# Sums of x's blocks pinned behind the steps for 1/rms, in a decoder step on one core

## The chip, the cores and the metric

The program runs on one core of one Trainium2 chip. The time is device microseconds of one execution, taken as the median of several runs. The engines are named as the profile names them: PE (TensorE) multiplies matrices, with PEld for the loading of its stationary operand; DVE (VectorE) and ACT (ScalarE) work on rows of 128 partitions; POOL (GpSimd) and SP (SyncE) here mostly issue DMAs. Matmul results arrive in PSUM and have to be read from there by DVE or ACT; everything else stands in SBUF.

## The reference

One inference step of a decoder with two layers, for 512 prompt tokens and 8 sample tokens at once, so 520 columns, model width 1024. Each layer is

```
x += 0.5 * swiglu(rms(x))
x += mixer(rms(x))          # pooling in layer 0, windowed attention in layer 1
x += 0.5 * swiglu(rms(x))

rms(x)    = x * rsqrt(mean(x*x) + 1e-5) * g
swiglu(h) = (silu(h @ w_gate) * (h @ w_up)) @ w_down        # 1024 -> 2816 -> 1024
```

So there are four feed-forward networks (FFN 0 to 3). Between FFN 1 and FFN 2 the keys and values are projected once from rms(x), with rotary positions on the keys. A final rms ends it. All numbers are float32.

## The kernel before

**Layout.** x is held transposed, as eight blocks of 128 channels by 520 tokens. Since 1/rms belongs to a token, and a token is a column, it can be multiplied in after a matrix product instead of before it: products are formed from x times g, and their result is multiplied by R, a tile that holds 1/rms of each token in all 128 partitions. So a product can start before R is known, but its result can't be used before.

**Matmuls.** Each float32 operand is split into a high and a low part (`split`, L238: ACT writes the high one at L242, DVE the low one at L243), and a product is made of three terms. Weights are split the same way (ACT L191, DVE L192) some pieces ahead of their use, and the columns go in two halves of 260. One matmul of the traces is 128 by 128 by 260.

**The two kinds of tile.** Each FFN makes 22 column tiles of the hidden width. A plain tile (`plain_tile`, 96 matmuls, L412) forms gate and up in two PSUM tiles, then DVE multiplies gate by R (L470), ACT takes silu, DVE multiplies by up (L472), and `hidden` splits the result for the down projection. A Strassen tile (`strassen_tile`, 84 matmuls, L437) needs seven products instead of eight. It needs sums and differences of x's blocks (`sums`, L515, in a dictionary `tt`, with parts th and tl), and sums of weights, for which a further piece S is loaded and added in by DMA and DVE (L155 to L165). The first `NPL[fi]` tiles of an FFN are plain, two in each; the sums of x's blocks are made meanwhile.

**1/rms.** The squares (ACT L363) are added up over x's eight blocks by DVE in `acc` (L367). `rstd_tok` multiplies acc by a column of ones on PE (L378), which gives the sum for each token, and then twelve DVE operations on 128 by 5 numbers (L382 to L389) make 1/rms from it by an initial guess and three Newton steps, as `r_tok`, one token to a partition. `rstd_all` spreads it over all partitions: DVE makes a diagonal matrix of r_tok's column (L397, L399), PE multiplies it by a matrix of ones (L398, L400), ACT copies the result to R (L401, L402).

**What sets the order.** Engines work off their queues in order, and run beside each other as semaphores let them. The order within a queue is made by a planner from a cost model when the program is built, except for instructions wrapped in `later`, which keep the place that the program gives them. In an FFN the steps above are called as hooks, one after each weight piece of the plain tiles (`start_hooks`, L592): a step of the sums, `rstd_tok`, `rstd_all`, then eight more steps of the sums.

**Elsewhere.** `kv_pass` runs the keys and then the values. During the keys it calls `rstd_tok` after block 1 and `rstd_all` after block 3, and the sums of FFN 2 are made during the values. `rope` (L821) turns the keys, in kv, and the queries, in attention: ACT copies the result out of PSUM (L825), DVE multiplies the PSUM result by cosines (L826), shuffles the copy, multiplies it by sines (L828) and adds. In attention `rstd_tok` and `rstd_all` stand between parts of the query projection. PSUM has four tiles of two banks each for all of this.

Of the kernel before, what the change touches and what calls it, by code (L numbers as in the profile page):

```python
# [28 lines left out]
LAG = 2  # L29
NPL = (2, 2, 2, 2)  # L30
HD = 64
# [178 lines left out]
def yoco_step(ctx, tc, ins, outs):  # L210
# [161 lines left out]
    def rstd_tok():  # L372
# [8 lines left out]
        t1 = cp.tile([P, 5], F32, tag="nt", name="nt")  # L381
        V.tensor_scalar(v, pss[:, :5], 1.0 / D, EPS, op0=ALU.mult, op1=ALU.add)  # L382
        V.tensor_scalar(y.bitcast(I32), v.bitcast(I32), 1, None, op0=ALU.arith_shift_right)
# [6 lines left out]

    def rstd_all(pool):

        dg2 = pool.tile([P, NS], F32, tag="dg2", name="dg2", bufs=1)
        pr, pr2 = pss_[0][:, 1, :], pss_[0][:, 0, 8 : 8 + NS]
        for t in range(4):
            dg = pool.tile([P, P], F32, tag="dg", name="dg", bufs=4)
            V.tensor_scalar(dg, ident, r_tok[:, t : t + 1], None, op0=ALU.mult)  # L397
            T.matmul(pr[:, t * P : (t + 1) * P], ones, dg, start=True, stop=True)  # L398
        V.tensor_scalar(dg2, ident[:, 112:120], r_tok[:, 4:5], None, op0=ALU.mult)  # L399
        T.matmul(pr2, ones, dg2, start=True, stop=True)  # L400
        S.copy(R[:, :SP], pr)  # L401
        S.copy(R[:, SP:], pr2)  # L402
# [48 lines left out]
    class Hidden(list):  # L451


        def __init__(self, tags):
            self.tags = tags

    def plain_tile(tmp, mov, hs, hooks):

        pg, pu = duo(), duo()
        for k0 in (0, 4):  # L460
            for banks in (pg, pu):
                w = W.get()
                W.prefetch()
                for k in range(k0, k0 + 4):
                    mm(w, k - k0, mov[k], banks, k == 0, k == KT - 1)
                if hooks:
                    hooks.pop(0)()
        g = tmp.tile([P, TOK], F32, tag="g", name="g")
        t = tmp.tile([P, TOK], F32, tag="t", name="t")
        V.tensor_tensor(halves(g), pg[:, :, :H], halves(R), op=ALU.mult)  # L470
        S.activation(t, g, AF.Silu)
        V.scalar_tensor_tensor(halves(g), pu[:, :, :H], -1.0, halves(t), op0=ALU.mult, op1=ALU.mult)  # L472
        hidden(g, hs)

# [40 lines left out]
    def sums(tmp, n, tt):  # L515


        for k in range(4):
# [7 lines left out]
            t1, t2, t3, t4 = hcols(t12, 0), hcols(t12, 1), hcols(t34, 0), hcols(t34, 1)  # L526
            V.tensor_tensor(t1, b11, b12, op=ALU.subtract)
            V.scalar_tensor_tensor(t2, t1, -1.0, b22, op0=ALU.mult, op1=ALU.subtract)
            tt[k] = pair(TT, [P, TOK])
            split(tt[k], t12)  # L530
            yield
            V.tensor_tensor(t3, b22, b12, op=ALU.subtract)
            V.scalar_tensor_tensor(t4, t2, -1.0, b21, op0=ALU.mult, op1=ALU.subtract)
# [57 lines left out]

    def start_hooks(tmp, n, tt):  # L592

        steps = sums(tmp, n, tt)
        step = lambda: next(steps, None)
        return [step, rstd_tok, lambda: rstd_all(tmp)] + [step] * 8


    mov1 = []
    with ff_pool() as tmp:  # L600
# [95 lines left out]

        ffn(0, tmp, mov0, start_hooks(tmp, 0, tt), tt, HH, deferred(1, tmp, "g", XX, mov1, TW), pool_prep())

# [97 lines left out]
    with ff_pool() as tmp:  # L796
# [11 lines left out]
        tt = {}  # L808
        ffn(1, tmp, mov2, start_hooks(tmp, 2, tt), tt, HH, deferred(N_KV, tmp, "g", XX, movk))

# [9 lines left out]
    def rope(out, banks, cosr, sinr, pool, tags):  # L820
# [4 lines left out]
        S.copy(halves(raw), banks[:, :, :H])  # L825
        V.tensor_tensor(halves(out), banks[:, :, :H], halves(cosr), op=ALU.mult)  # L826
        V.stream_shuffle(sw, raw, swap)
# [5 lines left out]
    with ff_pool() as tmp:  # L833
# [22 lines left out]
        def during_k(k):  # L856
            if k == 1:
                rstd_tok()
            if k == 3:
                rstd_all(tmp)  # L860

# [50 lines left out]
    with tc.tile_pool(name="at", bufs=2) as at:  # L912
# [158 lines left out]
        q_part(1, 0)  # L1071
        rstd_all(at)
        q_part(1, 1)
# [139 lines left out]
    with ff_pool() as tmp:  # L1213
# [29 lines left out]

        ffn(3, tmp, mov6, start_hooks(tmp, 5, tt), tt, HH, final_after)
        turn(*waiting.pop())
# [46 lines left out]
```

## Time and profile before

| | us |
|---|---|
| median of 3 runs | 1743.63 |
| lowest and highest run | 1741.86, 1750.61 |
| the profiled execution | 1745.72 |
| its span, first to last instruction | 1744.0 |
| mean granted TensorE clock in it | 0.973 |

The page of the profile gives the busy time of each engine and its share of the span, the span in 40 slices, and the chain of waits that ended last. The timeline lists single instructions or runs of the same one, with start, length and, in brackets, the idle time before it and what ended that. The windows view sums busy time by engine over a stretch. The granted clock is the share of full speed at which PE was let run; where it is 0.5, a matmul takes twice as long.

### The profile page before, as it was taken

To read this page: it belongs to the slowest core of one execution; us is meant where nothing else is said; L and a number is where in the kernel's file an instruction comes from. 1 tells how busy PE (TensorE), PEld (TensorE's weight loads), DVE (VectorE), ACT (ScalarE), POOL (GpSimd) and SP (SyncE) were. 2 spreads that over 40 slices of the span, in tenths; PEclk is the share of its full clock that TensorE was granted. 3 is DMA by queue.
4 is the path that set the end of the run, shared out by engine and by line. 5 is a ranking of instruction groups with operands and counts; after the bars stand their busy time and mean duration, and the time that the engine had idled before them with its cause. 6 is when DMAs were issued, how large, how long until landed. Compare 5 with 4: busy or idle time off the path is not lost.

```text
span 1744.0 us, 34399 instructions
## 1 busy us (share of the span) xinstructions
PE 1667.9 (96%) x13689; PEld 1655.0 (95%) x13689; DVE 1275.7 (73%) x2487; ACT 909.5 (52%) x1812; POOL 147.8 (8%) x180
## 2 busy tenths in 40 slices
PE   5999999999899999998999999998889899999996
PEld 5999999999899999998999999998879899999996
DVE  7775866878775875887775875888756785785775
ACT  6553643666552652654552643656766663463453
POOL 1001101001001101100101101100000110110100
PEclk8999999999899999998999999999979999999998
DMA  9445746653355755643645845642112465675621
GB/s 225 115 134 134 178 132 141 177 171 105 85 151 128 167 148 135 150 133 93 149 139 133 185 134 133 166 138 70 35 25 73 104 151 146 138 177 140 151 86 50
DMA packets 316687, 227.85 MB, mean 131 GB/s; under 512 B 9312, under 2 KB 291528, under 8 KB 316486
## 3 DMA queue, kind: packets, MB, share of 16 engines
q1 hardware_dynamic: 286400, 175.08, 35.2%
q0 software_dynamic: 23488, 42.34, 14.9%
q10 hardware_dynamic: 6638, 8.23, 1.5%
q8 instruction: 107, 1.75, 0.4%
q14 instruction: 54, 0.44, 0.1%
HBM read 181.16 MB, written 5.04 MB: 107 GB/s over the span
## 4 chain that ended last, share of the span: by engine, by line
PE 88%; DVE 6%; ACT 3%; DMA 2%; issue 1%; SPq 0%; ACTq 0%; DVEq 0%
PE ps L437 46%; PE ps L412 37%; DVE sm L990 1%; DVE wl L192 1%; PE ps L720 1%; PE ps L1046 1%; ACT sm L1005 1%; DMA pr<-in_bands_dram 1%; PE ps L745 1%; PE ps L378 0%; ACT wh L191 0%; PE ps L398 0%; DVE xl L243 0%; DMA S<-in_ffn_w_up_dram 0%; DVE tl L243 0%
## 5 line engine op out<-in xcount | busy, mean ns | idle before, releaser
L191 ACT ACTIVATE wh<-raw 128x512 fp32r<-128x512 f32 (+1 forms) x744 | 452.0, 623 | 566.7 <-PE ps L412 348.5
L192 DVE TENSOR_TENSOR wl<-raw,wh 128x512 fp32r<-128x512 f32 (+1 forms) x744 | 492.9, 678 | 219.5 <-ACT wh L191 209.7
L437 PE MATMUL ps<-tl,wh 128*128 128x260 f32 x1280 | 361.4, 282 | 0.0
L437 PE MATMUL ps<-th,wh 128*128 128x260 f32 x1280 | 360.9, 282 | 0.0
L437 PE MATMUL ps<-th,wl 128*128 128x260 f32 x1280 | 359.2, 282 | 0.0
L412 PE MATMUL ps<-hh,wh 128*128 128x260 f32 x1376 | 281.5, 285 | 3.6 <-DVE mx L990 2.2
L412 PE MATMUL ps<-hl,wh 128*128 128x260 f32 x1376 | 281.0, 283 | 0.0
L412 PE MATMUL ps<-hh,wl 128*128 128x260 f32 x1376 | 279.2, 283 | 0.0
L437 PEld LDWEIGHTS ps<-tl,wh 128*128 128x128 f32 x1280 | 241.0, 188 | 0.0
L437 PEld LDWEIGHTS ps<-th,wh 128*128 128x128 f32 x1280 | 240.8, 188 | 0.0
L437 PEld LDWEIGHTS ps<-th,wl 128*128 128x128 f32 x1280 | 240.1, 188 | 0.0
L412 PEld LDWEIGHTS ps<-hh,wh 128*128 128x128 f32 x1376 | 212.8, 189 | 5.0 <-DVE mx L990 2.9
L412 PEld LDWEIGHTS ps<-hl,wh 128*128 128x128 f32 x1376 | 214.8, 190 | 0.0
L412 PEld LDWEIGHTS ps<-hh,wl 128*128 128x128 f32 x1376 | 213.6, 189 | 0.0
L437 PE MATMUL ps<-xl,wh 128*128 128x260 f32 x720 | 201.6, 283 | 0.0
L437 PE MATMUL ps<-xh,wh 128*128 128x260 f32 x720 | 201.5, 282 | 0.0
L437 PE MATMUL ps<-xh,wl 128*128 128x260 f32 x720 | 197.5, 282 | 0.0
L156 POOL DMA_DIRECT2D raw<-raw x80 | 69.3, 866 | 1398.8 <-DVE wl L192 558.8
L571 DVE TENSOR_TENSOR u<-ps,R 128x520 f32<-128x520 f32 x96 | 67.1, 700 | 107.0 <-PE ps L412 107.0
L437 PEld LDWEIGHTS ps<-xl,wh 128*128 128x128 f32 x720 | 135.5, 188 | 0.0
L437 PEld LDWEIGHTS ps<-xh,wh 128*128 128x128 f32 x720 | 135.4, 188 | 0.0
L437 PEld LDWEIGHTS ps<-xh,wl 128*128 128x128 f32 x720 | 133.4, 188 | 0.0
(233 smaller groups left out, 2840.1 us busy)
## 6 DMA issues: line engine op xcount, KB each, us to landing
raw<-in_ffn_w_gate_dram SPq DMA_DIRECT2D x87, 512.0 KB, 4.0
raw<-in_ffn_w_up_dram SPq DMA_DIRECT2D x87, 512.0 KB, 5.8
raw<-in_ffn_w_down_dram SPq DMA_DIRECT2D x32, 1024.0 KB, 5.1
S<-in_ffn_w_up_dram SPq DMA_DIRECT2D x80, 256.0 KB, 5.5
raw<-raw POOLq DMA_DIRECT2D x80, 256.0 KB, 3.3
S<-raw POOLq DMA_DIRECT2D x80, 256.0 KB, 4.7
raw<-in_ffn_w_down_dram SPq DMA_DIRECT2D x16, 768.0 KB, 4.2
raw<-in_w_q_dram SPq DMA_DIRECT2D x8, 512.0 KB, 3.8
```

Source lines behind the costliest of these rows:

```text
L156: G.dma_start(blk(raw, 2, 1), blk(raw, 1, 1), accum_op=ALU.add)
L191: nc.scalar.activation(dh, src, AF.Copy)
L192: nc.vector.tensor_tensor(dl, src, dh.bitcast(F32), op=ALU.subtract)
L412: T.matmul(banks[:, hf, :H], a[:, kk, :], hcols(b, hf), start=(first and i == 0), stop=(last and i == 2),)
L437: T.matmul(bank[:, :H], a[:, kk, :], b, start=(not more and kk == 0 and i == 0), stop=(kk == 3 and i == 2), skip_group_check=more,)
L571: V.tensor_tensor(halves(u), banks[m][:, :, :H], halves(R), op=ALU.mult)
L720: T.matmul(o, a[:, s], b[:, kk, :], start=(n == 0), stop=(n == 5))
L745: T.matmul(po[:, half * 256 : half * 256 + 256], z[:, tau, c], b, start=(i == 0), stop=(i == len(lst) - 1),)
L990: V.tensor_tensor_reduce(out=sm[:, e * 256 : (e + 1) * 256], in0=self.pe[e][:, bi * 256 : (bi + 1) * 256], in1=cst[:, mk : mk + 256], op0= ...
L1005: S.activation(part(i), part(i), AF.Exp, bias=nm[:, i : i + 1], accum_out=den[:, i : i + 1])
L1046: T.matmul(po[:, bi * 256 : (bi + 1) * 256], a, p_[:, kc_], start=(n == 0), stop=(n == 3 * len(kts) - 1),)
```

## The change

1. FFN 0 has three plain tiles instead of two (so one Strassen tile less); the others keep two.
2. `later` pins the first of the twelve operations for r_tok, and the first subtract of each of the eight sums, in program order. In `start_hooks` the hook calls are rearranged: none for the first one or two weight pieces (`late`: 2 in FFN 0 and 1, 1 in FFN 3), then `rstd_tok` with a step of the sums behind it, none, `rstd_all`, and the other seven steps.
3. `rstd_all` makes no diagonal. r_tok's column, repeated 128 times along the free axis, is the stationary operand, and the identity the moving one. 25 DVE operations go.
4. A plain tile that ends before `rstd_all` was called is copied out of PSUM by ACT (two copies), and its remaining steps, as operations from SBUF, are put off until R is known. In the built program that holds for the first tile of FFN 0 and the first of FFN 1.
5. In `rope` the product with the cosines reads ACT's copy instead of PSUM.

```diff
-NPL = (2, 2, 2, 2)
+NPL = (3, 2, 2, 2)
...
-        V.tensor_scalar(v, pss[:, :5], 1.0 / D, EPS, op0=ALU.mult, op1=ALU.add)
+        later(V.tensor_scalar(v, pss[:, :5], 1.0 / D, EPS, op0=ALU.mult, op1=ALU.add))
...
-    def rstd_all(pool):
+    def rstd_all():
-        dg2 = pool.tile([P, NS], F32, tag="dg2", name="dg2", bufs=1)
         pr, pr2 = pss_[0][:, 1, :], pss_[0][:, 0, 8 : 8 + NS]
         for t in range(4):
-            dg = pool.tile([P, P], F32, tag="dg", name="dg", bufs=4)
-            V.tensor_scalar(dg, ident, r_tok[:, t : t + 1], None, op0=ALU.mult)
-            T.matmul(pr[:, t * P : (t + 1) * P], ones, dg, start=True, stop=True)
-        V.tensor_scalar(dg2, ident[:, 112:120], r_tok[:, 4:5], None, op0=ALU.mult)
-        T.matmul(pr2, ones, dg2, start=True, stop=True)
+            T.matmul(
+                pr[:, t * P : (t + 1) * P], r_tok[:, t : t + 1].broadcast_to([P, P]), ident, start=True, stop=True
+            )
+        T.matmul(pr2, r_tok[:, 4:5].broadcast_to([P, P]), ident[:, 112:120], start=True, stop=True)
         S.copy(R[:, :SP], pr)
         S.copy(R[:, SP:], pr2)
...
+    copied, there = [], [False]
+
+    def known():
+        there[0] = True
+        while copied:
+            copied.pop(0)()
...
         g = tmp.tile([P, TOK], F32, tag="g", name="g")
         t = tmp.tile([P, TOK], F32, tag="t", name="t")
-        V.tensor_tensor(halves(g), pg[:, :, :H], halves(R), op=ALU.mult)
-        S.activation(t, g, AF.Silu)
-        V.scalar_tensor_tensor(halves(g), pu[:, :, :H], -1.0, halves(t), op0=ALU.mult, op1=ALU.mult)
-        hidden(g, hs)
+        if not there[0]:
+            S.copy(halves(g), pg[:, :, :H])
+            S.copy(halves(t), pu[:, :, :H])
+
+            def rest():
+                V.tensor_tensor(g, g, R, op=ALU.mult)
+                S.activation(g, g, AF.Silu)
+                V.scalar_tensor_tensor(g, t, -1.0, g, op0=ALU.mult, op1=ALU.mult)
+                hidden(g, hs)
+
+            copied.append(rest)
+        else:
+            V.tensor_tensor(halves(g), pg[:, :, :H], halves(R), op=ALU.mult)
+            S.activation(t, g, AF.Silu)
+            V.scalar_tensor_tensor(halves(g), pu[:, :, :H], -1.0, halves(t), op0=ALU.mult, op1=ALU.mult)
+            hidden(g, hs)
...
-            V.tensor_tensor(t1, b11, b12, op=ALU.subtract)
+            later(V.tensor_tensor(t1, b11, b12, op=ALU.subtract))
...
-            V.tensor_tensor(t3, b22, b12, op=ALU.subtract)
+            later(V.tensor_tensor(t3, b22, b12, op=ALU.subtract))
...
-    def start_hooks(tmp, n, tt):
+    def start_hooks(tmp, n, tt, late):
         steps = sums(tmp, n, tt)
         step = lambda: next(steps, None)
-        return [step, rstd_tok, lambda: rstd_all(tmp)] + [step] * 8
+        there[0] = False
+        none = lambda: None
+
+        def norm():
+            rstd_tok()
+            step()
+
+        def norm_all():
+            rstd_all()
+            known()
+
+        return [none] * late + [norm, none, norm_all] + [step] * 7
...
-        ffn(0, tmp, mov0, start_hooks(tmp, 0, tt), tt, HH, deferred(1, tmp, "g", XX, mov1, TW), pool_prep())
+        ffn(0, tmp, mov0, start_hooks(tmp, 0, tt, 2), tt, HH, deferred(1, tmp, "g", XX, mov1, TW), pool_prep())
...
-        ffn(1, tmp, mov2, start_hooks(tmp, 2, tt), tt, HH, deferred(N_KV, tmp, "g", XX, movk))
+        ffn(1, tmp, mov2, start_hooks(tmp, 2, tt, 2), tt, HH, deferred(N_KV, tmp, "g", XX, movk))
...
         S.copy(halves(raw), banks[:, :, :H])
-        V.tensor_tensor(halves(out), banks[:, :, :H], halves(cosr), op=ALU.mult)
+        V.tensor_tensor(out, raw, cosr, op=ALU.mult)
...
-        ffn(3, tmp, mov6, start_hooks(tmp, 5, tt), tt, HH, final_after)
+        ffn(3, tmp, mov6, start_hooks(tmp, 5, tt, 1), tt, HH, final_after)
```

In kv and in attention only the calls of `rstd_all` lose their argument; the pin inside `rstd_tok` and the spread act there too.

More of the change, by code (lines that the diff above doesn't have):

```diff
@@ L859, in during_k @@
             if k == 3:
-                rstd_all(tmp)
+                rstd_all()
         mov3, tt = [], {}
@@ L1071, in yoco_step @@
         q_part(1, 0)
-        rstd_all(at)
+        rstd_all()
         q_part(1, 1)
```

## The prediction

> **What bounds the kernel now.** I read the page first, then the chain of waits, then the timeline and windows of the places where TensorE (PE) stands idle.
>
> ```profile
> PE 1667.9 (96%) x13689; PEld 1655.0 (95%) x13689; DVE 1275.7 (73%) x2487; ACT 909.5 (52%) x1812; POOL 147.8 (8%) x180
> PEclk8999999999899999998999999999979999999998
> PE 88%; DVE 6%; ACT 3%; DMA 2%; issue 1%; SPq 0%; ACTq 0%; DVEq 0%
> ```
>
> PE is busy 96% of the span and holds 88% of the chain that ended last. So there are two ways to gain: fewer matmuls, or fewer of the remaining idle stretches. One stretch of the chain gives the price of a matmul when nothing waits:
>
> ```profile
> 55.55 54.53 PE ps L437 x456
> ```
>
> 54.53/456 = 0.1196 us. A Strassen tile (84 matmuls) costs 10.05 us, a plain tile (96) 11.48.
>
> The idle lies at the starts: where 1/rms is formed and spread before the first plain tile's result may be scaled. Timeline of the first FFN (start, length, engine, operation; in brackets the idle before it and its releaser):
>
> ```profile
> 33.34 0.63 ACT L191 ACTIVATE wh<-S 128x512 fp32r<-128x512 f32 x1 [4.60 <-DMA S<-raw]
> 37.11 0.70 DVE L367 TENSOR_TENSOR acc<-acc,sq 128x520 f32<-128x520 f32 x1
> 37.95 2.26 PE L378 MATMUL ps<-ones,acc 128*128 128x1 f32 x10 [9.93 <-DVE acc L367]
> 55.39 0.28 PE L437 MATMUL ps<-xh,wh 128*128 128x260 f32 x1
> ```
>
> PE stands 9.93 us (from 28.02) for the sum of squares. That sum is late because ACT, with the last squares queued behind, waits 4.60 us for a weight sum S by DMA, which only a Strassen tile needs. The other starts:
>
> ```profile
> 430.68 1.17 PE L378 MATMUL ps<-ones,acc 128*128 128x1 f32 x10
> 444.49 2.04 PE L398 MATMUL ps<-dg,ones 128*128 128x128 f32 x8 [6.78 <-ACT th L242]
> 447.50 0.80 PE L412 MATMUL ps<-xh,wh 128*128 128x260 f32 x2 [0.74 <-ACT R L402]
> 455.98 0.28 PE L437 MATMUL ps<-xh,wh 128*128 128x260 f32 x1
> ...
> 807.76 2.05 PE L398 MATMUL ps<-dg,ones 128*128 128x128 f32 x8 [6.44 <-ACT th L242]
> ...
> 1382.09 2.05 PE L398 MATMUL ps<-dg,ones 128*128 128x128 f32 x8 [3.96 <-issue]
> 1392.56 0.28 PE L437 MATMUL ps<-xh,wh 128*128 128x260 f32 x1
> ```
>
> ACT's th is named as releaser, but PE really waits for the DVE chain that makes r_tok, since DVE mixes the twelve tiny steps with the sums of x's blocks:
>
> ```profile
> 431.89 0.17 DVE L382 TENSOR_SCALAR nv<-ps 128x5 f32<-128x5 f32 x1
> 437.48 0.70 DVE L243 TENSOR_TENSOR tl<-t,th 128x520 fp32r<-128x520 f32 x1
> 438.09 0.16 DVE L387 SCALAR_TENSOR_TENSOR nt<-nt,nv 128x5 f32<-128x5 f32 x1
> 438.16 0.43 DVE L528 SCALAR_TENSOR_TENSOR t<-t,xb 128x260 f32<-128x260 f32 x1
> 438.50 0.43 DVE L532 TENSOR_TENSOR t<-xb,xa 128x260 f32<-128x260 f32 x1
> 443.59 0.17 DVE L389 SCALAR_TENSOR_TENSOR r_tok<-nt,ny 128x5 f32<-128x5 f32 x1
> ...
> 1178.94 0.15 DVE L382 TENSOR_SCALAR nv<-ps 128x5 f32<-128x5 f32 x1
> 1181.15 0.17 DVE L389 SCALAR_TENSOR_TENSOR r_tok<-nt,ny 128x5 f32<-128x5 f32 x1
> ```
>
> The chain lasts 11.87 us in the second FFN, and 2.38 in attention where hardly anything stands between. The same rows give DVE's pace: 0.61 from a long operation to the next, 0.34 from a short one.
>
> How much of each start is waiting, by the windows view (length; busy time and count by engine; granted clock; DMA share; GB/s):
>
> ```profile
> core 0: us, PE busy (x) PEld busy (x) DVE busy (x) ACT busy (x) POOL busy (x), PEclk, DMA share, GB/s
> 28.00:56.00 28.00, 17.33 (x123) 17.24 (x123) 20.66 (x52) 14.57 (x25) 2.64 (x3) 0.76 0.45 97
> 419.00:456.00 37.00, 29.47 (x216) 29.20 (x216) 29.67 (x78) 21.58 (x37) 3.69 (x5) 0.82 0.30 67
> 794.00:843.00 49.00, 41.82 (x326) 41.47 (x325) 31.05 (x70) 21.67 (x39) 7.45 (x10) 0.90 0.51 119
> 1367.00:1393.00 26.00, 21.30 (x156) 21.02 (x155) 18.82 (x50) 14.97 (x25) 2.60 (x3) 0.87 0.41 93
> ```
>
> At 0.1196 each, 216, 326 and 156 matmuls are 25.8, 39.0 and 18.7 us; the windows last 11.2, 10.0 and 7.3 longer. That bounds what these three starts can give back, lost clock included.
>
> **A gap also costs clock.** The pooling step shows what follows a short one, and the change leaves short ones:
>
> ```profile
> 386.07 0.28 PE L720 MATMUL ps<-tl,xh 128*128 128x256 f32 x1
> 390.58 1.25 PE L378 MATMUL ps<-ones,acc 128*128 128x1 f32 x10 [2.70 <-DVE acc L367]
> 392.25 0.42 PE L720 MATMUL ps<-th,xh 128*128 128x256 f32 x1
> 390.00:395.00 5.00, 4.42 (x26) 4.45 (x27) 2.86 (x15) 3.00 (x10) 1.77 (x2) 0.70 0.78 257
> ```
>
> After 2.70 us of idle the same matmul takes 0.42 instead of 0.28 and the clock of the window is 0.70, so 0.30 x 5 = 1.5 us are lost there; with what spills into the next window I take 1.7 for each start that keeps a gap. [...]
>
> **The change, part by part.**
>
> First FFN. With a third plain tile the early weights need no S, so the 4.60 us wait of ACT goes from ahead of the squares. By the order in which the changed program was built, what stands before the last square is two weight splits and one copy of a finished tile; I put the last square at about 29.5, acc at 30.6 and L378 at 30.75, an idle of 2.7 instead of 9.93. Then L378 (1.17), 31 matmuls, the spread (1.03), 161 matmuls: 192 x 0.1196 = 23.0, and Strassen starts at 55.9, against 55.39. But one more of the 22 tiles is done by then: 10.05 - 0.5 = 9.6 gained, less the clock of 1.7: **7.9**. The 12 more matmuls are in it. The 31 matmuls (3.7 us) cover the r_tok chain (2.4). Sums follow the chain on DVE, by my count done at 57 to 59, about when product two asks for them; 3 us later would cost 3: ends 5 and 9.6.
>
> The copying: ACT takes both results of a tile out before R is known, four copies in two tiles, each about
>
> ```profile
> 794.30 0.57 ACT L825 COPY rp<-ps 128x520 f32<-128x520 f32 x1
> 1188.12 0.70 DVE L826 TENSOR_TENSOR qT<-ps,xh 128x520 f32<-128x520 f32 x1
> 1188.73 0.69 DVE L828 TENSOR_TENSOR rp<-rp,xl 128x520 f32<-128x520 f32 x1
> ```
>
> 0.57, one of them ahead of the last square (counted). It frees the PSUM banks early, so PE need not stop for R. The product that finishes the tile later, and rope's first product, read SBUF instead of PSUM: 0.69 against 0.70, nothing. In rope the keys' banks come free with the copy, without R.
>
> Spread without the diagonal: five times 5 DVE operations go, all off PE's path once DVE is not late, so nothing by themselves. The stationary operand is now one column repeated 128 times. No row shows such a load. Nearest:
>
> ```profile
> L398 PEld LDWEIGHTS ps<-dg,ones 128*128 128x128 f32 x40 | 7.3, 273 | 17.7 <-issue 10.8 <-ACT th L242 7.0
> ```
>
> 273 ns now. I take the same; if it were free the 40 would give 7.3 at most (all exposed), if twice as slow cost 10.9 more.
>
> Second FFN. The pin holds L382 and its eleven successors ahead of the sums: 431.9 + 2.4 + one long operation = r_tok at 434.9, instead of 443.59. PE has 49 matmuls (5.9 us) behind L378, to 437.7: no wait for R, and without waits it reaches Strassen at 444.2 instead of 455.98. Now the sums are late: behind r_tok DVE has 15 short and 21 long operations plus 1.0 of small copies of the sinks, 15 x 0.34 + 21 x 0.61 + 1.0 = 18.9, to 453.8, with the last ACT hop 455.4. PE gets 36 to 48 matmuls in meanwhile, waiting for one sum after the other. At 456.9 I count 60 Strassen matmuls where before had 8: 52 x 0.1196 = 6.2, less 1.7: **4.5**. Ends: 2 if the sums come 2.5 later, 11.2 if they never count.
>
> Keys and values. 103 matmuls (12.3 us) now lie between L378 and the spread, so the idle goes: up to 10.0. But the third weight piece's low part stands on DVE behind cs, kT and rp, two each at 0.61 and over, which wait for R (about 809.4): ready at 814.3, while PE asks at 811.1: 3.2 back, and 1.7 of clock: **5.1**. Ends 2 and 10. The chain itself isn't shortened here; 14 other operations still stand between its steps.
>
> Attention: the spread comes after 50 matmuls instead of 57; PE had no wait there, so R 0.9 earlier may shorten what waits for it: 0.5, ends -2 and 3.
>
> Fourth FFN. r_tok at 1368.1 + 3.0 = 1371.1 instead of 1381.5; 15 short and 22 long (18.5), 2.8 of waits for R and banks and one ACT hop put the last sum at about 1393.4. PE would be there at 1385.2. At 1394.4 I count 48 done against 15: 3.9 - 1.7 = **2.2**. Ends 0 and 7.3.
>
> What the pin adds as a wait: DVE stands at L382 for PE, with all sums and weight low parts behind it. Before, that wait was
>
> ```profile
> 795.49 0.17 DVE L382 TENSOR_SCALAR nv<-ps 128x5 f32<-128x5 f32 x1 [0.37 <-PE ps L378]
> ```
>
> 0.37, and L378 keeps its place in PE's order in every start (96 matmuls before it in both FFNs with 96 before), so I count the same. Queues: SP issues one DMA less and POOL two less, nothing else is moved past another there.
>
> Sum: 7.9 + 4.5 + 5.1 + 0.5 + 2.2 = 20.2. The profiled execution took 1745.72, so 1725.5; it lies 2.1 above the median of the runs (1743.63), so **1723** in terms of the median. Own range of this case 1717 to 1730.
>
> **Rivals.** (1) The short gaps leave the clock alone, or are shorter than I think. Four times 1.7 comes back: gain 27.0, 1716.6. For it: no row shows where below 2.70 us the loss begins, and my gaps may come out shorter; against: the row of 390.58. [...] (2) DVE becomes the bound in the starts: every sum also needs an ACT pass between its DVE steps (th, about 0.6) which DVE exposes when it has nothing else. Four sums by 0.87 make 3.5 more in each of three starts, 10.4: gain 9.8, 1734. For it: DVE is busy 29.67 of 37 us in 419 to 456; against: weight work lies between to fill the hops. (3) The planner's order makes nothing of it: what is gained in a start is taken back by the next weight's wait (DMA share 0.45 in 28 to 56, so no bound is near): 1743. (4) Slower: DVE stands at L382 while PE is late at L378, with the sums and the low parts of the weights that PE needs next behind it. Each start then ends d later, where d is that wait. It turns the sign at d = 20.2/4 = 5.1 us and shows as slower from (20.2 + 8.7)/4 = 7.2; at the 9.93 of today's first gap, 4 x 9.93 = 39.7, less 20.2: 1763. Against: the 0.37 above, and no row of the other starts with an idle before L378.
>
> **How the numbers follow.** The forecast gets 0.58, rival 1 0.15, 2 0.15, 3 0.05, 4 0.07. Half a per cent, about what a measurement can tell, is 8.7 us: faster is below 1734.9. That takes nearly all of the forecast (0.57) and of rival 1 (0.15), and over half of rival 2 (0.09): 0.81; same 0.12, slower 0.07. The range 1712 to 1737 takes in the forecast's ends, rival 1 whole and most of rival 2; about 0.84 is inside.
>
> **What would show it.** In the first FFN: idle of about 2.7 ahead of L378, no wait of ACT for S ahead of the squares, Strassen first at 56 with one tile less behind it. In all starts: r_tok's chain 2.4 to 3 us long except in the keys, no idle ahead of the spread. At Strassen's start of the second and fourth FFN short PE waits for tl, in all some 5 to 10 us; in the values a wait near 3 for a weight's low part. Rival 1 shows as clock 1.0 in those windows, rival 2 as DVE idle with ACT th as releaser, rival 4 as a long idle of DVE ahead of L382. I am wrong if the new waits at Strassen's start equal the old ones at the spread, or if the repeated column's load is far above 273 ns.

## The result, and the profile after

The changed kernel took 1725.75 us in the median of five runs (1724.41 to 1730.32), the kernel before 1741.86 in five runs beside them: a ratio of 0.9906, 95% interval 0.9876 to 0.9935. That is 16.1 us. The forecast was 1723, from a gain of 20.2. The profiled execution of the changed kernel has a span of 1728.0 against 1744.0.

The page of the changed kernel, engines' busy time and the granted clock over the span:

```profile
PE 1669.6 (97%) x13701; PEld 1654.0 (96%) x13701; DVE 1269.1 (73%) x2454; ACT 904.7 (52%) x1810; POOL 146.1 (8%) x178
PEclk9999999999999999999999999999979999999998
```

The 12 more matmuls are there, and three slices of the clock that were 8 before (the first, the 11th and the 19th: the starts of the first and second FFN and of the keys) are 9. The timeline of PE shows where the waits went (start, length, then in brackets the idle ahead and its releaser):

```profile
30.31 1.28 PE L378 MATMUL ps<-ones,acc 128*128 128x1 f32 x10 [2.56 <-DVE acc L367]
35.23 1.05 PE L395 MATMUL ps<-ident,r_tok 128*128 128x128 f32 x8
55.74 0.28 PE L435 MATMUL ps<-xh,wh 128*128 128x260 f32 x1
...
447.47 0.80 PE L435 MATMUL ps<-th,wh 128*128 128x260 f32 x2 [2.63 <-ACT th L242]
...
1370.30 0.39 PE L435 MATMUL ps<-xh,wl 128*128 128x260 f32 x1 [0.81 <-DVE wl L192]
1375.89 0.51 PE L435 MATMUL ps<-th,wh 128*128 128x260 f32 x2 [1.04 <-ACT th L242]
```

No spread (now L395) has an idle ahead of it. The first FFN's idle went from 9.93 to 2.56. In the second and fourth FFN the idle did not go away; a smaller one now stands behind the spread, where Strassen asks for the sums and for parts of weights. The windows view shows how much that costs, over the first Strassen run of the second and then the fourth FFN. Before:

```profile
455.98:510.65 54.67, 54.67 (x460) 54.67 (x459) 46.38 (x80) 34.03 (x67) 5.23 (x6) 1.00 0.60 141
1392.56:1447.25 54.69, 54.69 (x460) 54.69 (x459) 46.46 (x80) 34.18 (x67) 5.25 (x6) 1.00 0.57 140
```

After:

```profile
436.38:500.02 63.64, 59.00 (x460) 57.25 (x459) 54.08 (x96) 39.71 (x77) 5.23 (x6) 0.95 0.48 121
1366.70:1428.64 61.94, 58.50 (x460) 56.90 (x459) 52.15 (x94) 38.08 (x76) 5.25 (x6) 0.97 0.50 124
```

The same 460 matmuls took 54.67 and 54.69 without any wait before, and take 63.64 and 61.94 now, at a lower clock: 9.0 and 7.3 us paid back there. PE is idle for 4.6 and 3.4 us of them (length less busy time); the lower clock is part of the rest. Of that idle 2.0 and 1.3 us end with a weight's high or low part (ACT L191, DVE L192), most of the remainder with a sum.

From the starts of the same matmuls in both traces one can sum up the lead of the changed kernel. At the end of the first FFN's first Strassen run it is 9.69 us (110.09 against 100.40); at the second FFN's L378, after the pooling step, 8.06; at the end of that FFN's first Strassen run 10.63; at the L378 in the keys still 10.63; at the end of FFN 2's first Strassen run 19.88; at the fourth FFN's L378, after attention, 18.18; at the end of its first Strassen run 18.61; at the last L378 15.64; over the span 16.0. So the four starts gave 9.69, 2.57, 9.25 and 0.43, 21.9 in all, and 6 were lost where the change does little or nothing: 1.6 in pooling, 1.7 in attention, the rest behind the fourth FFN.

### The profile page after: what moved, and what is told of

The parts are those of the page before. It is cut to its first block, busy times and chain, and to the rows that moved or that the text cites. A ratio compares the mean times of both kernels' runs of the same rounds, so it can differ in the third digit from the quotient of the medians.

```text
span 1728.0 us, 34367 instructions
## 1 busy us (share of the span) xinstructions
PE 1669.6 (97%) x13701; PEld 1654.0 (96%) x13701; DVE 1269.1 (73%) x2454; ACT 904.7 (52%) x1810; POOL 146.1 (8%) x178
## 4 chain that ended last, share of the span: by engine, by line
PE 67%; DVE 4%; ACT 3%; issue 0%; ACTq 0%; DVEq 0%
PE ps L435 35%; PE ps L410 30%; ACT sm L1034 1%; DVE sm L1019 1%; PE ps L1075 1%; DVE wl L192 1%; PE ps L1159 0%; PE ps L1052 0%; DVE xl L243 0%; ACT xh L242 0%; PE ps L1127 0%; DVE rp L856 0%; ACT wh L191 0%; PE ps L1250 0%; ACT oT L1087 0%
## 5 line engine op out<-in xcount | busy, mean ns | idle before, releaser
L191 ACT ACTIVATE wh<-raw 128x512 fp32r<-128x512 f32 (+1 forms) x742 | 449.6, 621 | 542.8 <-PE ps L410 326.3
L192 DVE TENSOR_TENSOR wl<-raw,wh 128x512 fp32r<-128x512 f32 (+1 forms) x742 | 491.0, 677 | 206.9 <-ACT wh L191 202.2
```

What stands on the lines that cost most here:

```text
L191: nc.scalar.activation(dh, src, AF.Copy)
L192: nc.vector.tensor_tensor(dl, src, dh.bitcast(F32), op=ALU.subtract)
```

## The experiments

The same four places are used for each kernel. A is the end of the first FFN's first Strassen run from the start of the span. B, C and D are the times from L378 to the end of the next first Strassen run, for the second FFN, for keys and values with FFN 2, and for the fourth FFN. They are differences of times in the timelines of one profiled execution each; the ratio is to the kernel before, from runs beside each kernel. The runs come from four batches, and the kernel before had a median of 1741.86 beside the first execution of the changed kernel, 1745.48 beside again, npl2, rope_psum and pin_rms_only, 1747.15 beside unpin_f1, best, npl3_before and late1, and 1744.73 beside the other four. So kernels of different batches are better compared by their ratios than by their medians.

```
                            A       B       C       D    median    ratio [95% interval]
before                   110.09   79.97  103.67   80.34
changed                  100.40   77.40   94.42   79.91  1725.75   0.9906 [0.9876, 0.9935]
again                    104.05   77.10   94.43   79.91  1727.42   0.9899 [0.9875, 0.9924]
npl2                     119.47   77.26   94.48   79.77  1739.67   0.9963 [0.9948, 0.9978]
rope_psum                101.75   77.66  100.20   79.96  1735.37   0.9938 [0.9918, 0.9958]
pin_rms_only             107.80   69.70   96.21   80.33  1724.96   0.9882 [0.9865, 0.9899]
unpin_f1                 103.25   69.69   94.40   79.57  1719.16   0.9835 [0.9820, 0.9850]
best                     102.29   69.69   94.40   74.31  1712.63   0.9795 [0.9779, 0.9812]
npl3_before              108.70   79.87  103.58   80.37  1749.18   1.0007 [0.9996, 1.0018]
late1                    104.07   75.13   94.43   80.40  1722.60   0.9850 [0.9828, 0.9871]
diag                     102.37   77.12   94.71   78.85  1729.44   0.9910 [0.9890, 0.9931]
rope_only                110.71   79.96   94.77   81.24  1743.11   0.9990 [0.9975, 1.0004]
best_nocopy1             102.11   78.07   94.40   74.31  1720.04   0.9855 [0.9831, 0.9879]
best_nocopy0             102.26   69.71   94.39   74.31  1713.80   0.9814 [0.9790, 0.9837]
```

**The changed kernel once more (again).**

> The changed kernel once more, unaltered. In its first profile it was 8.06 us ahead at the second FFN's L378 after 9.65 ahead at pooling's, lost another 2.5 after the gap of 3.29 us near the end, and 1.7 in attention. If these losses are the clock's answer to the same gaps, and that depends on where a gap happens to fall, the granted clock behind pooling's gap, behind the gap near the end and behind the first FFN's 2.56 us gap is different from execution to execution: at least one of these three places changes by 1.5 us or more, while the places without a gap agree within 0.2. Rival: the changed order causes the losses; then all three come out as in the first profile, 1.6 and 2.5 lost and nothing in the first FFN.

The places where PE has no idle of 2 us or more at once agree: C 94.42 and 94.43, D 79.91 twice. Of the places with such a gap, two don't. Pooling, from the first matmul of the first FFN's last Strassen run to the second FFN's L378, took 144.61 in the first execution and 143.02 in this one (before: 142.99), so the 1.6 us "lost" there were not lost this time. The first FFN, which had got away free in the first execution, paid here. This execution's L378 in the timeline, and the windows from L378 to the end of the first Strassen run, of the first execution and then of this one:

```profile
30.90 2.22 PE L378 MATMUL ps<-ones,acc 128*128 128x1 f32 x10 [2.59 <-DVE acc L367]
...
30.31:100.40 70.09, 70.09 (x586) 70.09 (x587) 60.05 (x117) 44.74 (x84) 7.88 (x9) 1.00 0.57 137
...
30.90:104.05 73.15, 73.15 (x586) 73.15 (x587) 60.32 (x117) 45.20 (x84) 7.86 (x9) 0.95 0.55 133
```

Same 586 matmuls, no idle in either, 3.1 us apart by the granted clock alone. Attention, from its L378 to the fourth FFN's, went from 191.55 to 187.48. The gap near the end cost less too: from the matmul behind it to the last L378 it took 34.64 us, 35.48 in the first execution and 33.01 before. So two of the three places changed by 1.5 us or more, as the theory has it, and the third by 0.84; what pooling and attention "lost" in the first comparison is not the change's doing as far as two executions can tell.

**Two plain tiles in the first FFN (npl2).**

```diff
-NPL = (3, 2, 2, 2)
+NPL = (2, 2, 2, 2)
```

> Two plain tiles in the first FFN as before, all else as changed. My theory: the first FFN's gain is the third tile, because the weight sum S is then not waited for by ACT ahead of the squares: ACT waits for S again, PE's idle ahead of L378 goes from 2.6 back to 6 to 10 us, the first FFN ends 5 to 9.7 later, the kernel takes some 7 more; all later stages as in the changed kernel. Rival: the pin on the sums alone brings the squares forward: the idle stays at about 3, and the loss is under 2.5.

A is 119.47: 19 us later than in the first execution of the changed kernel, and 9.4 later than before the change. The timelines of ACT and PE:

```profile
36.18 0.63 ACT L191 ACTIVATE wh<-S 128x512 fp32r<-128x512 f32 x1 [8.35 <-DMA S<-raw]
...
38.80 2.29 PE L378 MATMUL ps<-ones,acc 128*128 128x1 f32 x10 [10.93 <-DVE acc L367]
...
66.28 0.80 PE L435 MATMUL ps<-th,wh 128*128 128x260 f32 x2 [2.63 <-ACT th L242]
```

ACT waits 8.35 us for S with the last squares behind it, and since the sums now come after r_tok, PE waits for them too (2.63 us in the last row). The theory holds for the idle (a little above its range), and was too small for the stage: without the third tile the rest of the change makes this FFN slower than before.

**Rope's product from PSUM (rope_psum).**

```diff
-        V.tensor_tensor(out, raw, cosr, op=ALU.mult)
+        V.tensor_tensor(halves(out), banks[:, :, :H], halves(cosr), op=ALU.mult)
```

> Only rope's first product reads PSUM again. I had costed this edit at nothing (0.69 against 0.70). Theory now: it holds the keys' PSUM banks until R is known, so in keys and values the spread comes 48 matmuls behind L378 instead of 103, and PE waits there again: idle of 4 to 7 us ahead of the spread and 0.7 for R, 6 to 9 of that stage's 9.25 gained are lost, the rest unchanged within 0.3 but for clock. Rival: the gain in that stage comes from the pins and the spread; then it stays above 7.

C goes from 94.42 to 100.20, 5.8 lost, a little under the expected 6 to 9. The timeline of PE:

```profile
795.68 1.58 PE L395 MATMUL ps<-ident,r_tok 128*128 128x128 f32 x8 [3.25 <-DVE r_tok L389]
798.23 0.80 PE L410 MATMUL ps<-xh,wh 128*128 128x260 f32 x2 [0.74 <-ACT R L400]
```

The waits for r_tok and for R are back, the first at 3.25 (4 to 7 were expected) instead of the 6.44 before: the chain from L382 to r_tok took 9.02 us here and 11.25 before, and no diagonal stands between r_tok and the spread. A, B and D stay, but for the clock.

**The pins on the sums off (pin_rms_only).**

```diff
-            later(V.tensor_tensor(t1, b11, b12, op=ALU.subtract))
+            V.tensor_tensor(t1, b11, b12, op=ALU.subtract)
...
-            later(V.tensor_tensor(t3, b22, b12, op=ALU.subtract))
+            V.tensor_tensor(t3, b22, b12, op=ALU.subtract)
```

> The pins on the sums' subtracts are gone, that on L382 stays. The planner then puts 18, 30, 30 and 36 other operations of DVE between the first and last step of r_tok in the four starts (changed kernel 11, 12, 24, 13, own steps included). Theory: the pins on the sums hold the chain together; in the fourth FFN the chain takes 10 us or more again and PE waits 3 us or more ahead of the spread, in the second FFN the spread comes behind the first product. Against the changed kernel the second FFN changes by -2 to +4 (its sums come earlier, R later), the fourth by 0 to +5, the first by 0 to +3, the kernel by +1 to +8. Rival: the sums are what comes last in the second and fourth FFN; unpinned they are ready earlier and the kernel gets 2 to 5 faster.

The kernel came out at 1724.96, with the changed kernel at 1727.42 beside it: no slower, though the expectation had it so. The stages show two large effects of opposite sign. A is 107.80, more than the expected 0 to 3 later. The work for the sums stands between the squares again, on ACT, whose last square starts at 31.34 instead of 28.61, and on DVE between the adds:

```profile
34.80 2.26 PE L378 MATMUL ps<-ones,acc 128*128 128x1 f32 x10 [6.88 <-DVE acc L367]
```

B is 69.70 instead of 77.40, far outside what was expected (-2 to +4). Windows from L378, of this kernel and then of the changed one:

```profile
428.56:498.26 69.70, 68.91 (x576) 68.56 (x575) 63.70 (x135) 47.86 (x93) 7.91 (x9) 1.00 0.59 131
...
422.62:500.02 77.40, 72.76 (x576) 71.01 (x575) 65.47 (x135) 47.97 (x93) 7.92 (x9) 0.96 0.49 118
```

Both hold 576 matmuls; 576 x 0.1196 is 68.9. Unpinned, PE loses almost nothing in the second FFN, although r_tok's chain takes 9.66 us there instead of 2.86. The pins on the sums are what costs there, as the rival had it. No run takes off the pin on L382, so its own share is not shown.

**The pins off in the second FFN alone (unpin_f1).** As the run before, with the pins kept in the first FFN, in keys and values and in the fourth:

```diff
     def sums(tmp, n, tt):
+        keep = later if n in (0, 3, 5) else (lambda ins: ins)
...
-            later(V.tensor_tensor(t1, b11, b12, op=ALU.subtract))
+            keep(V.tensor_tensor(t1, b11, b12, op=ALU.subtract))
...
-            later(V.tensor_tensor(t3, b22, b12, op=ALU.subtract))
+            keep(V.tensor_tensor(t3, b22, b12, op=ALU.subtract))
```

> The changed kernel, but in the second FFN alone the subtracts of the sums are not pinned. With all those pins gone that FFN took 69.70 us from L378 to the end of its first Strassen run, against 77.40 and 77.10 in two executions of the changed kernel and 79.97 before, while the first FFN lost its gain. Theory: pinned, the sums start only after r_tok and come last, each through ACT and back; unpinned they come first and R comes late, which harms nothing, because the copies have freed the PSUM banks. Expected: this stage 69 to 71, the first FFN as changed (70 to 73), the kernel 6 to 8 us below the changed one. Rival: the 7.5 us were the order elsewhere, in the first FFN's late end above all; then the stage stays above 75 and the kernel within 2.

B is 69.69, A 103.25, C 94.40: each place keeps the better of the two. The kernel's ratio is 0.9835 against 0.9906 and 0.9899; by the medians it is 6.6 below the first 1725.75, as expected, by the ratios 11 to 12. The stage itself gave 7.4 to 7.7.

**Three plain tiles in the fourth FFN too (best).** To the run before:

```diff
-NPL = (3, 2, 2, 2)
+NPL = (3, 2, 2, 3)
```

> As the run before, and three plain tiles in the fourth FFN too, there with the pins. Theory: in the fourth FFN too the sums come last (79.91 us from L378 to the end of its first Strassen run, of which 587 matmuls are 70.2 at 0.1196); a third plain tile costs 12 matmuls (1.44) and gives the sums 11.5 us more: the stage takes 73 to 76 to the same point (one tile less in the run counts as done), the kernel 3 to 6 less than the run before, 10 to 13 below the changed one. Rival: the wait there is for the weights' own low parts on DVE, which are as many with a plain tile; then the stage is 1.4 longer or the same.

D falls from 79.57 to 74.31. Windows of its second and fourth FFN from L378:

```profile
422.99:492.68 69.69, 68.87 (x576) 68.55 (x575) 63.95 (x135) 47.84 (x93) 7.92 (x9) 1.00 0.56 131
1334.93:1409.24 74.31, 74.31 (x623) 74.31 (x622) 62.00 (x120) 46.80 (x86) 7.80 (x9) 1.00 0.56 136
```

In the fourth PE is busy all 74.31 us at full clock. (The same window of the changed kernel, 1348.73 to 1428.64, holds 611 matmuls, not the 587 of the expectation; 12 more make the 623.) The kernel is at 1712.63, a ratio of 0.9795 to the kernel before: faster than both, and more than twice the change's own gain.

**Three plain tiles alone (npl3_before).** The kernel before with

```diff
-NPL = (2, 2, 2, 2)
+NPL = (3, 2, 2, 2)
```

> The kernel before with three plain tiles in the first FFN, nothing else. My prediction gave the first FFN's gain to this edit (ACT's wait for S goes). With two tiles and all else changed the first FFN ended later than before (119.47 against 110.09 to the same matmul), and without the pins the idle ahead of L378 was 6.87 with three. Theory: the third tile alone takes a part off that idle (9.93 to 5 to 7), but R is late again and waited for: the first FFN gains 0 to 4, all other stages nothing, kernel 0 to 4 faster. Rival, as predicted: the tile does it alone, idle 2.5 to 3.5, 7 to 10 gained.

A is 108.70, 1.4 gained, the kernel the same (1.0007). The timeline of PE:

```profile
34.02 2.27 PE L378 MATMUL ps<-ones,acc 128*128 128x1 f32 x10 [6.88 <-DVE acc L367]
46.58 0.51 PE L412 MATMUL ps<-xh,wh 128*128 128x260 f32 x2 [0.74 <-ACT R L402]
```

The idle is 6.88, the same as with the pins off: taking ACT's wait for S away gives 3 of the 7.4 us of shorter idle, and pinning the sums behind the squares, with the third tile there, the other 4.3.

**No copying out (late1).**

```diff
-        ffn(0, ..., start_hooks(tmp, 0, tt, 2), ...)
+        ffn(0, ..., start_hooks(tmp, 0, tt, 1), ...)
...
-        ffn(1, ..., start_hooks(tmp, 2, tt, 2), ...)
+        ffn(1, ..., start_hooks(tmp, 2, tt, 1), ...)
```

> The changed kernel with the hooks of the first and second FFN one weight piece earlier, so that R counts as known when their first tile ends and that tile is not copied out; PE's order is almost the same. Theory: PSUM's four tiles are not enough for tile one, the rstd tile and tile two, so PE waits in the middle of tile two until R is there and DVE has emptied a bank of tile one: 2 to 6 us of idle there in each of the two FFNs, the kernel 3 to 10 slower than the changed one, nothing elsewhere. Rival: the copies only move work from DVE to ACT; the same within 1.5.

Nothing was lost: A 104.07, B 75.13, kernel 1722.60, a ratio of 0.9850 where the changed kernel has 0.9906 and 0.9899. PE stops for R only in the second FFN:

```profile
434.05 0.51 PE L410 MATMUL ps<-xh,wh 128*128 128x260 f32 x2 [1.15 <-ACT R L400]
```

1.15 us, and the FFN was still 2 us shorter than with copies (75.13 against 77.10 and 77.40). This edit also moves the sums a weight piece earlier, which may be what pays; the two weren't taken apart, and the stages show only these 2 us of what the ratio gained. The theory falls for pinned sums; the rival is nearer.

**No copying, with the sums of the second FFN unpinned (best_nocopy1).** This is the kernel of best with the second of late1's edits.

> The fastest version so far (sums of the second FFN not pinned, three plain tiles in the first and fourth), with the hooks of the second FFN one weight piece earlier so that its first tile is not copied out. With pinned sums that cost nothing (75.1 against 77.4 for the stage). Theory: unpinned sums make R late, and only the copies make that harmless: the spread goes back to 48 matmuls behind L378 and PE waits for R again: idle of 5 to 8 us there, stage 76 to 80 instead of 69.7, kernel 6 to 10 slower than that version. Rival: the unpinned order alone does it, and the stage stays below 72.

```profile
435.93 2.08 PE L395 MATMUL ps<-ident,r_tok 128*128 128x128 f32 x8 [6.10 <-DVE r_tok L389]
438.98 0.80 PE L410 MATMUL ps<-xh,wh 128*128 128x260 f32 x2 [0.74 <-ACT R L400]
```

Here the copies carry it: B is 78.07 instead of 69.69, and PE waits 6.10 for r_tok ahead of the spread, much as the 6.78 before the change. (Here too the edit moves the sums a weight piece earlier; it did not help.) The kernel takes 6.2 more than the version of the next run, which ran beside it and keeps these copies.

**No copying in the first FFN (best_nocopy0).** This is the kernel of best with the first of late1's edits.

> The fastest version with the hooks of the first FFN one weight piece earlier, so that its first tile is not copied out. There the sums are pinned and R comes early. Theory: the copies aren't needed in this place: end of the first Strassen run 100 to 104.5 as in the other executions with or without them, the spread among them being the clock's, kernel within 2 of that version. Rival: the copy ahead of the last square is what keeps the first FFN from ending earlier; without it L378 comes 0.5 earlier and the kernel gains.

A is 102.26 against 102.29, and the kernel 1713.80 against 1712.63: no difference that these runs can tell.

**The diagonal back (diag).** The changed kernel with `rstd_all` as it was before.

> The changed kernel with the diagonal matrix back in the spread, so 25 operations of DVE more. In the built order the spread stands 3, 10, 3 and 5 matmuls later behind L378 in the four starts and 7 in attention. Theory: with the chain pinned the diagonals are off the path: kv and the first FFN unchanged within 0.3 but for clock, the second and fourth FFN 0 to 1.2 longer because DVE's sums, the last there, are pushed 1.1 back each; the kernel 0 to 3 slower. The load of the stationary operand is 273 ns in both forms. Rival: the spread carries a good part of the gain; 4 or more slower.

A, B and C agree with the changed kernel's within 0.3 but for the clock. D is 1.1 lower at 78.85, against the expectation, and the sums there are not pushed back; 0.9910 against 0.9906 is no difference. In attention, though, PE waits 6.15 us for a softmax tile that it waits 2.06 for in the changed kernel; the next experiment has the same wait.

The load of the repeated column, which no row of before showed, takes as long as that of a diagonal. Here are the loads in the view that groups instructions: of the changed kernel, of this run, and of the kernel before in the windows 1181 to 1190 and 440 to 448.

```profile
L395 PEld LDWEIGHTS ps<-ident,r_tok 128*128 128x128 f32 x40 | 4.9, 190 | 0.0
...
L398 PEld LDWEIGHTS ps<-dg,ones 128*128 128x128 f32 x40 | 4.9, 191 | 0.0
...
L398 PEld LDWEIGHTS ps<-dg,ones 128*128 128x128 f32 x8 | 1.0, 191 | 0.0
...
L398 PEld LDWEIGHTS ps<-dg,ones 128*128 128x128 f32 x8 | 1.8, 327 | 7.0 <-ACT th L242 7.0
```

It is 190 ns against 191, none of it waited for. The 273 ns of the prediction and of the expectation above is a mean over two clocks: before, three of the five spreads stood behind an idle and ran at a granted clock of 0.50 (from 444.46, 807.73 and 1382.06), where a load took 327 to 329 ns in the mean, and two ran at 1.00 with 191. The one spread of the repeated column that stands behind a long idle, at 435.93 of best_nocopy1, took 2.08 us on PE where it takes 1.05 in the changed kernel; the diagonals behind an idle took 2.04 and 2.05 before.

**Rope's product alone (rope_only).** The kernel before with the one line of `rope` changed.

> The kernel before with rope's first product reading ACT's copy, nothing else. Undoing this edit in the changed kernel cost 5.8 of the 9.2 us gained in keys and values. Theory: it frees the keys' banks without R, so the spread goes 126 matmuls behind L378 and no wait for R is left there even without the pins: 7 to 9.3 gained from L378 to the end of the first Strassen run (103.67 before, so 94.4 to 96.7), all else unchanged, kernel 5 to 10 faster. Rival: it needs the pins, because the sums and low parts of weights are late without them; then under 5 gained.

C is 94.77: 8.9 of the 9.25 us come from this one line, with no pin. Windows from L378 of the keys, this kernel and then before:

```profile
795.04:889.81 94.77, 93.88 (x782) 92.98 (x781) 76.92 (x150) 54.58 (x106) 12.57 (x16) 1.00 0.59 143
...
794.28:897.95 103.67, 96.49 (x782) 96.14 (x781) 77.54 (x150) 55.63 (x106) 12.68 (x16) 0.95 0.54 130
```

But the kernel as a whole took only 0.1% less (interval -0.25 to +0.04%). In this profile 3.4 us of it went in attention (193.22 from L378 to the fourth FFN's, 189.84 before), where the queries use rope as well, and about 3 behind it. The 3.4 has a cause in the trace: PE waits for the softmax tile sm, in this kernel and then before:

```profile
1200.13 0.69 PE L1023 MATMUL ps<-ident,sm 128*128 128x128 f32 x2 [6.15 <-DVE sm L1013]
...
1204.50 0.33 PE L1023 MATMUL ps<-ident,sm 128*128 128x128 f32 x1 [0.87 <-ACT sm L1011]
```

Over the whole of attention PE is idle for 19.8 us here and 16.6 before. The same wait of 6.15 stands in diag, where PE is idle for 20.0. So with the product from SBUF the old spread costs some 3 us in attention that the new one does not, which is a use of the third edit that neither the prediction nor the expectations had. Attention came out at 193.22 and 192.20 in the two kernels that have both the diagonal and the product from SBUF, and between 184.70 and 191.55 in the others, but by 4 us apart in two executions of one kernel too, with idle times of 16.8 and 17.2. Of the 3 us behind attention 0.9 stand in D (81.24 against 80.34) and 2.1 behind a gap of 3.29 us near the end: from the matmul behind it to the last L378 it took 35.11 us here, and 33.01 before, where the clock in that stretch was 1.00. Why the runs show not even the remaining 5 us stays open.

## Why the prediction was right, and where it wasn't

**The size of the whole** was right: 16.1 measured, 20.2 forecast, by the case that was held likeliest. The starts gave 21.9 in the compared profiles where 19.7 was forecast. But three of the five terms were off, one too small by 4.2 and two too large by 1.6 to 1.9 each, and the first one goes up and down with the clock. That the errors nearly cancel in the sum is luck.

**First FFN, forecast 7.9.** L378 at 30.31 (30.75 forecast), the idle 2.56 (2.7), Strassen at 55.74 (55.9). The gain was 9.69 in an execution in which the clock held, and A of the six kernels whose first FFN is the changed kernel's own (changed, again, rope_psum, unpin_f1, best, best_nocopy1) has a mean of 102.3, which is 7.8 below 110.09. That is right in size, the 1.7 for the clock included, though no single execution has to pay just that. The step was wrong in what it put it down to: "With a third plain tile the early weights need no S, so the 4.60 us wait of ACT goes from ahead of the squares" is half of it. Alone that edit left 6.88 of idle and gained 1.4; the pins that keep the sums behind the squares' adds take the rest; and the rest of the change without the third tile loses 9.4, since ACT waits for S again and PE reaches Strassen before the sums. The gain is the two together.

**Second FFN, forecast 4.5, measured 2.6 and 2.9** (79.97 to 77.40 and 77.10). r_tok was early and Strassen was reached at 436.38, that is 13.8 behind L378 where 13.5 was forecast. The step that was too small is "to 453.8, with the last ACT hop 455.4", or 24.7 behind L378. The last tl ran from 449.19 to 449.89, 27.3 behind L378, and of the 60 Strassen matmuls counted to 456.9 (448.84 here) 47 were done. The timeline of DVE in the changed kernel says why:

```profile
445.08 0.70 DVE L243 TENSOR_TENSOR tl<-t,th 128x520 fp32r<-128x520 f32 x1 [0.70 <-ACT th L242]
...
447.45 0.70 DVE L243 TENSOR_TENSOR tl<-t,th 128x520 fp32r<-128x520 f32 x1 [0.24 <-ACT th L242]
...
449.19 0.70 DVE L243 TENSOR_TENSOR tl<-t,th 128x520 fp32r<-128x520 f32 x1 [0.70 <-ACT th L242]
```

DVE stands and waits for ACT's th before each of the last three low parts, 1.64 us, and for 0.58 before an earlier one: rival 2's mechanism, at 2.2 us, where the sums came 2.6 later than forecast. PE's waits for parts of weights, 2.0 us, were in no term either. More than this size, the sign of the pins was missed: "The pin holds L382 and its eleven successors ahead of the sums" was counted as the gain, when R early was worth nothing there once the copies had freed the banks (best_nocopy1, without them, waits 6.10). Unpinned with copies the stage takes 69.7, 10.3 below before.

**Keys and values, forecast 5.1, measured 9.25.** "PE asks at 811.1: 3.2 back" did not happen. The changed trace has PE busy 93.58 of the 94.42 us from L378 to the end of the Strassen run, with the clock at 1.00:

```profile
783.65:878.07 94.42, 93.58 (x782) 92.94 (x781) 77.20 (x145) 54.84 (x106) 12.71 (x16) 1.00 0.59 143
```

The low part came when I said, at 803.29 for 0.68 (814.3 less the lead of 10.63 is 803.7), but PE didn't stop: it had 87 matmuls of the values left behind the spread (10.4 us at 0.1196), and PE's next wait for a result of DVE comes only at 808.62, behind them; the forecast let it run dry after some 2 us of them. With no gap there was no clock to lose, so the 1.7 was wrong too. "Up to 10.0" was the right reading of the window. And rope's edit, "nothing" by its duration, is what carried it: its worth was in whom it sets free, not in what it takes. The forecast named that ("the keys' banks come free with the copy, without R") without giving it the gain.

**Attention, forecast 0.5.** Measured from -1.7 to +2.4 in two executions; not resolved.

**Fourth FFN, forecast 2.2, measured 0.4** in both executions. "48 done against 15" was too good: 42 were done at that point, and the run took 61.94 in all instead of 54.69. PE got to Strassen when forecast (1366.70, with the lead of 18.18 at 1384.9 of before, where 1385.2 was forecast). The last sum came later, at 1378.31, which is 1396.5 of before against 1393.4. Of PE's 3.4 us of idle there 1.5 end with a sum and 1.3 with a part of a weight, for which the step had no term. A further plain tile removes all of it (best, 74.31).

**The rivals.** Rival 1 is neither right nor wrong: the clock was lost behind most gaps of 2.6 to 2.7 us and not behind all. That decides against taking 1.7 as a fixed price. Behind the 2.56 us ahead of the first L378 the changed kernel kept a clock of 1.00; behind 2.59 its second execution had 0.95 over the same matmuls, which took 73.15 us instead of 70.09. Behind 2.60 in best_nocopy1 two matmuls took 0.64 us from 32.48 to 35.08 where they take 0.40 in the changed kernel, and A was 102.11. The nine executions with the third tile and the pins in the first FFN have an A of 100.40 in one, 101.75 to 102.37 in five and 103.25 to 104.07 in three: 1.4 to 2.0 and 2.9 to 3.7 more than the first. Rival 2 was part of the truth in the second FFN. Rival 3 did not happen as a whole, since B and C stay gained, but the waits for parts of weights named above are its mechanism. Rival 4 did not either. The wait of DVE for L378 was not the 0.37 of before in each start, as counted, but 1.37, 1.57, 0.37 and 1.06, far from the 5.1 at which it would turn the sign. The longest:

```profile
423.83 0.17 DVE L382 TENSOR_SCALAR nv<-ps 128x5 f32<-128x5 f32 x1 [1.57 <-PE ps L378]
```

## What to carry to other kernels

When two results compete for one engine, ask which of them the busy engine needs first in that stage, and whether a buffer copied out makes the other harmless. The same pins on the sums gained some 5 us in the first FFN (107.80 without them against a mean of 102.3) and cost 7.5 in the second. An edit that costs nothing by its duration may still be the one that frees a buffer, so follow who waits for the banks. And look at a gain stage by stage: large effects of opposite sign hide in a total that has not moved.

## What the hardware did that I had not expected

The clock's answer to a gap is not fixed. Near the end both kernels have the same gap of 3.29 us with the same code behind it. Timeline and windows of before:

```profile
1697.29 0.66 PE L1221 MATMUL ps<-ident,xg 128*128 128x128 f32 x4 [3.29 <-ACT xg L1239]
...
1695.00:1700.00 5.00, 2.71 (x23) 2.71 (x24) 3.85 (x9) 2.94 (x6) 0.00 (x0) 1.00 0.00 0
1700.00:1705.00 5.00, 5.00 (x44) 5.00 (x44) 2.74 (x6) 1.85 (x4) 0.00 (x0) 1.00 0.01 3
```

and of the changed kernel:

```profile
1679.18 1.11 PE L1250 MATMUL ps<-ident,xg 128*128 128x128 f32 x4 [3.29 <-ACT xg L1268]
...
1677.00:1682.00 5.00, 2.82 (x13) 2.82 (x14) 3.75 (x9) 2.94 (x6) 0.00 (x0) 0.62 0.00 0
1682.00:1687.00 5.00, 5.00 (x33) 5.00 (x32) 0.70 (x3) 0.82 (x2) 0.00 (x0) 0.69 0.02 5
```

Full clock in one, 0.62 and 0.69 in the other. Over the time in which PE was busy that is 0.38 x 2.82 + 0.31 x 5.00 = 2.6 us for the same gap. In the changed kernel the granted clock was 0.50 from 1678.24 to 1685.07. Over the 10 us from the first matmul behind this gap the clock was 1.00 before, 0.86 in again, 0.83 in best and pin_rms_only, and 0.71 in npl2 and in the changed kernel. From that matmul to the last L378 it took 33.01 us before, 34.64 in again, 35.11 in rope_only and 35.48 in the changed kernel. What decides between these outcomes is not shown by the runs.

For a prediction it means that each gap of the size seen here (2.56 to 3.29 us) carries a loss that the profile of another execution does not fix, 0 to 2.6 us near the end and 0 to 3.1 in the first FFN, and that two kernels compared by one profile each can differ by that much without the change being the cause.
